# Block-sum copies on SyncE's queue, one y store, earlier sums in a hybrid decoder block

## The chip, the cores and the metric

The kernel runs on one core of a Trainium2 chip. The metric is the device time of one execution in microseconds (us). TensorE (PE) multiplies; VectorE (DVE), ScalarE (ACT) and GpSimd (POOL) do the element-wise work; SyncE (SP), ACT and POOL issue transfers (DMA) between DRAM and the core's memory, or between two places in DRAM.

## The reference

```python
h = concat(meta_tokens, x)                                  # 16 + 1024 tokens, 1024 wide
n = rmsnorm(h, norm_g)
u, z_pool, q, k, v, z_attn, f, g_pool, g_attn = split(n @ w_in[0])
y_pool = causal_multiscale_pool(u, pool_w, pool_scale) * silu(z_pool)      # 4 groups of 128, windows 2, 4, 8, 16
log_f  = log_sigmoid(f + b_forget)
y_attn = forgetting_attention(q, k, v, log_f) * silu(z_attn)               # 8 heads of 64, causal softmax
merged = sigmoid(g_pool) * (y_pool @ w_up_pool[0]) + sigmoid(g_attn) * (y_attn @ w_up_attn[0])
out = rmsnorm(h + merged @ w_out[0], final_norm_g)[16:]
```

All arrays are float32. The kernel keeps that precision by splitting each operand into a high and a low part and adding three products (high x high, high x low, low x high).

## The kernel before, in words

Work runs in stages: loading and normalising x (to about 20 us), the first q, k and v projections (to 60), attention merged with projections (64 to 430), a product of blocks of h with columns of w_in in seven block products instead of eight (430 to 550), the up projections (to 637), and the output projection, again in seven block products (to 714).

**Attention** has 16 units: head pairs p = 0 to 3, head e of a pair, half of the queries. A unit with 5 or 9 key blocks computes scores and adds the forget term (`L710`, `L715`), takes the maxima with a transpose at `L729`, and then for each key block subtracts the maximum, takes the exponential (`L752`), splits it into `ph` and `pl` (`L756`, `L757`) and multiplies with V (`L775`). The scores of the next unit stand among the soft blocks of this one. Between those steps PE works on projections that nothing waits for yet: `f_u(3, 2, 1, 0)`, then eight `gp` and four `ga` columns (`f_raw`). Each loads a raw weight of 512 KB (`raw`, `L151`), splits it into `whi` (ACT, `L156`) and `wlo` (POOL, `L158`), multiplies (`L170`) and evicts its result through `st` (ACT, `L357` and `L347`) to DRAM (`sp_u`, `sp_gp`, `sp_ga`, by SP). The pool of `st` has two buffers: an eviction into it waits until the store of the one but last has landed.

**Block sums.** The two stages with seven products need sums of blocks: TD of w_out (512x512), GS of w_in (512x768) and HS of h, where hi and lo parts are added or the negated block (`neg`) is subtracted. They are built in DRAM while attention runs: a copy puts one block in place (`put`, pieces of 512 KB), and an accumulating DMA that POOL issues adds another (`add`, `L616`). The table `SUMS` says after which unit's transposes which copies are queued and which add is issued. ACT issues the copies, in `move` (`L612`), between an exponential and the following `ph`; in the soft blocks of a unit its queued copies are spread. SP stores the negated blocks (`L609`), the sums of exponentials (`accd`, `L607`) and, at a unit's end, the two halves of the unit's output `t` as `y` and `y2` (`L788`, 128 KB each). When both heads of a pair are done, POOL adds `y2` to `y` (`add_y`, `L643`). The sum of p = 0 is issued at i = 5, of p = 1 at i = 9, of p = 2 at i = 13.

**Order.** PE's order is written by hand. The order on ACT, DVE, POOL and SP is set when the program is built, from the dependencies and from `after(...)` and `behind(...)`; each engine then works its list strictly in order, and each queue of DMAs likewise starts them in order. An instruction waits by semaphores for what it reads and for the buffers that it writes. DMAs share a small set of semaphores, so a DMA's issue can also wait for an earlier DMA that used the same one.

Of the kernel before, what the change touches and what calls it, by code (L numbers as in the profile page):

```python
# [8 lines left out]
F32 = mybir.dt.float32  # L9
# [7 lines left out]
SEQ = 1024  # L17
# [9 lines left out]
COL_U, COL_Z, COL_Q, COL_K, COL_V, COL_ZA = 0, 512, 1024, 1536, 2048, 2560  # L27
# [17 lines left out]
def r32(ap):  # L45
    return ap.bitcast(F32)
# [7 lines left out]
def tile_hybrid_block(ctx, tc, x, meta, norm_g, w_in, b_forget, pool_w, pool_scale,  # L54
# [84 lines left out]
    def tt(out, x, y, op, eng):  # L139
        if eng is nc.gpsimd:  # L140
            pool_tt(out, x, y, op)
        else:
            eng.tensor_tensor(out, x, y, op=op)

    los = []

    def split_w(srcs, pool=None, tags=("wh", "wl")):
        raw = wp.tile([128, KO, 128], F32, name="raw")
        k0 = 0
        for s in srcs:  # L150
            nc.sync.dma_start(raw[:, k0:k0 + s.shape[1], :], s)  # L151
            k0 += s.shape[1]
        hi = (pool or wp).tile([128, KO, 128], F32R, name="whi", tag=tags[0])
        lo = (pool or wp).tile([128, KO, 128], F32R, name="wlo", tag=tags[1])
        for k in range(0, KO, 4):
            nc.scalar.activation(hi[:, k:k + 4], raw[:, k:k + 4], AF.Copy)  # L156
# [83 lines left out]
    def rows(e):  # L240
        return slice(64 * e, 64 * e + 64), slice(64 - 64 * e, 128 - 64 * e)
# [230 lines left out]
    for n, (kind, t0, t1) in enumerate(todo):  # L472
        if n + 4 < 8:
            xts[n + 4] = norm_load(n + 4)
        if kind == "q":
            run(q_piece(0, wq, t0, t1))
        elif kind == "k":
            run(k_piece(0, wk, t0, t1))
        else:
            g = v_piece(0, wv, t0, t1)  # L480
            run(g)
        i = {0: 2, 1: 3, 3: 4, 4: 5, 5: 8, 6: 6, 7: 7}.get(n)
        if i is not None:
            norm_t(i, xts[i], ntok(i))
        if n == 0:
            hv_ = split_hi(rv, gp, "g")
            wv = split_lo(rv, hv_, gp, "g")
            VT[0] = gp.tile([128, L], F32, name="vt", tag="g")
            v_alloc(0)
        i = {1: 4, 2: 5, 3: 8, 4: 6, 5: 7}.get(n)  # L490
        if i is not None:
            norm_scale(xts[i], ntok(i), norm_stat(xts[i], ntok(i)))
        if n == 2:
            zero_q(0)
        if n == 4:
            wf = at_.tile([128, KO, H], F32, name="wf", bufs=1)
            nc.sync.dma_start(wf, w_in2[:, :, COL_F:COL_F + H])
        if n == 8:
            wfs = at_.tile([128, KO, 2 * H], F32R, name="wfs", bufs=1)
            nc.vector.tensor_copy(wfs[:, :, :H], wf)  # L500
            nc.vector.tensor_tensor(wfs[:, :, H:], wf, r32(wfs[:, :, :H]), op=ALU.subtract)
        if n in (4, 7, 10):
            run(v_blocks(0, *range(max(1, 2 * (n // 3) - 2), 2 * (n // 3))))
    G_.close()
# [71 lines left out]
    TD = {n: dr.tile([512, 512], F32, name=f"td{n}") for n in (1, 2, 3, 4, 5)}  # L576
    WB = {"11": w_out[0][:512, :512], "12": w_out[0][:512, 512:], "21": w_out[0][512:, :512], "22": w_out[0][512:, 512:]}

    GS = {n: dr.tile([512, 768], F32, name=f"gs{n}") for n in (1, 2, 3, 4, 5)}
    GB = {f"{r + 1}{c + 1}": (w_in[0][512 * r:512 * r + 512, z:z + 512], w_in[0][512 * r:512 * r + 512, g:g + 256])  # L580
          for r in range(2) for c, (z, g) in enumerate(((COL_ZA, COL_GA + 512), (COL_Z, COL_GA + 768)))}
    for j in range(4, 8):
        spill["ga", j] = dr.tile([128, SEQ], F32, name=f"sp_ga{j}")
    HS = {n: dr.tile([512, 512], F32, name=f"hs{n}") for n in ("11", "22", "l11", "l22", "A", "B", "C", "X")}

    accs = []

    def hblock(d, blk):
        r, c = int(blk[0]) - 1, int(blk[1]) - 1
        return r32(d[c][:, :, 512 * r:512 * r + 512])  # L590

    def rows_of(t):
        return t.rearrange("(k p) c -> p k c", p=128)

    puts, held, negs = [], [], []

    def put(dst, src):
        for r in (0, 256):
            puts.append((dst[r:r + 256], src[r:r + 256]))

    def put_g(dst, src):
        put(dst[:, :512], src[0])
        puts.append((dst[:, 512:], src[1]))

    def move(u, b):
        if b == 2 and held:
            nc.sync.dma_start(*held.pop(0))  # L607
        while b == 3 and negs:
            nc.sync.dma_start(*negs.pop(0))  # L609
        if b:  # L610
            for _ in range(-(-len(puts) // (u.nb - b))):
                after(nc.scalar.dma_start(*puts.pop(0)), exps[-1])  # L612

    def add(dst, src):
        d, r = [t.rearrange("r c -> (r c)").rearrange("(p m) -> p m", m=2048) for t in (dst, src)]
# [1 line left out]

    trs = []

    def put_h(n):  # L620
        for d, h in ((HS[n], hh4), (HS["l" + n], hl4)):
            for k in (0, 2):
                puts.append((rows_of(d)[:, k:k + 2], hblock(h, n)[:, k:k + 2]))

    def put_neg(blk, k, *dsts):
        t = ap_.tile([128, 512], F32, name="neg", bufs=1)
        after(nc.scalar.activation(t, hblock(hh4, blk)[:, k], AF.Copy, scale=-1.0), exps[-1])
        for c in range(0, 512, 256):
            sub = nc.gpsimd.tensor_tensor(t[:, c:c + 256], t[:, c:c + 256], hblock(hl4, blk)[:, k, c:c + 256],
                                          op=ALU.subtract)  # L630
            after(sub, accs[-1])
        for d in dsts:
            negs.append((HS[d][128 * k:128 * k + 128], t))

    def n21(k):
        put_neg("21", k, "X", "A")

    def n12(k):
        put_neg("12", k, "C")

    def add_y(p):
        d, r = [spill[n, p].rearrange("(p k) c -> p (k c)", k=2) for n in ("y", "y2")]
        behind(nc.gpsimd.dma_start(d, r, accum_op=ALU.add, max_dma_last_dim=8192), trs[-1])  # L643
# [18 lines left out]

    def sums_of(i):
# [11 lines left out]
    class Unit:  # L675
# [69 lines left out]
        def soft(self, b):  # L745
# [4 lines left out]
                self.acc = ap_.tile([KB, 512], F32, name="acc", bufs=2)  # L750
            nc.vector.tensor_tensor(s[:kb, c0:], s[:kb, c0:], self.pm[:kb, c0:], op=ALU.subtract)  # L751
            exps.append(nc.scalar.activation(s[:kb, c0:], s[:kb, c0:], AF.Exp))  # L752
# [3 lines left out]
            nc.scalar.activation(ph[:kb, c0:], s[:kb, c0:], AF.Copy)  # L756
# [33 lines left out]

    def merged(a, c):
# [697 lines left out]
```

## Time and profile before

| what | us |
|---|---|
| median of the runs | 721.78 (721.3 to 722.93) |
| profiled execution | 722.44, of it span 720.4 |
| mean granted clock of PE in it | 0.996 |
| PE busy | 707.4 (98% of the span) |
| DVE, ACT, POOL busy | 512.0 (71%), 425.9 (59%), 353.9 (49%) |

The span runs from the first to the last instruction of the profiled execution; its own time is 2.04 longer. A row of a timeline reads: start, duration, engine and line, operation with output and inputs, shape, count, and in brackets the idle time in front of it with what ended it. An engine name with q (ACTq, SPq) is that engine's issue of a DMA, not the transfer. Durations of matmuls include their pipeline, so consecutive ones overlap.

### The profile page before, as it was taken

What the parts mean: (1) busy time and instruction counts of PE and PEld (TensorE: products, weight loads), DVE (VectorE), ACT (ScalarE), POOL (GpSimd) and SP (SyncE); (2) the same over time, 40 slices, a digit from 0 to 9 for tenths busy, and PEclk for the clock granted to TensorE, in tenths of its full rate; (3) what the DMA queues carried; (4) which work ended last, traced back from release to release, by engine and by line L of the source; (5) the groups of instructions that cost most, each with busy time, mean ns of one, the idle gap of its engine ahead of it and who ended that gap; (6) DMA issues with size and microseconds to landing.
All of it is one profiled execution on the core that took longest, in us unless ns stands there. A gap on an engine that the chain in (4) does not pass through costs nothing.

```text
span 720.4 us, 10921 instructions
## 1 busy us (share of the span) xinstructions
PE 707.4 (98%) x3613; PEld 610.7 (85%) x3613; DVE 512.0 (71%) x909; ACT 425.9 (59%) x936; POOL 353.9 (49%) x481
## 2 busy tenths in 40 slices
PE   8999999799999999999999999999999999999996
PEld 6997999798889988898888888888888888888885
DVE  5743488477688767787587866899847545888775
ACT  7753577567787867777587614455646332535445
POOL 5412336477377675747388643458951010007152
PEclk9999999999999999999999999999999999999999
DMA  9211225986968889497858768799518366861006
GB/s 308 65 30 30 60 62 199 271 244 193 260 177 230 239 229 281 118 261 214 224 154 206 223 202 318 239 304 308 129 35 273 113 224 233 272 224 60 0 1 233
DMA packets 97482, 134.09 MB, mean 186 GB/s; under 512 B 11809, under 2 KB 63009, under 8 KB 95154
## 3 DMA queue, kind: packets, MB, share of 16 engines
q1 hardware_dynamic: 83296, 94.07, 40.8%
q0 software_dynamic: 2512, 18.35, 13.3%
q10 hardware_dynamic: 11618, 20.98, 8.2%
q8 instruction: 28, 0.46, 0.2%
q14 instruction: 28, 0.23, 0.1%
HBM read 103.29 MB, written 62.59 MB: 230 GB/s over the span
## 4 chain that ended last, share of the span: by engine, by line
PE 94%; ACT 2%; DMA 2%; DVE 1%; issue 1%; POOL 0%; POOLq 0%; ACTq 0%
PE pj L170 55%; PE pj L1049 12%; PE pj L1369 8%; PE po L775 5%; PE pt L1049 4%; PE pt L1369 2%; PE ps L711 2%; DMA sp_u<-st 2%; PE ps L710 2%; PE pj L521 1%; PE pt L232 1%; PE pj L711 1%; PE pj L710 1%; ACT qa L268 1%; PE pn L232 0%
## 5 line engine op out<-in xcount | busy, mean ns | idle before, releaser
L170 PE MATMUL pj<-hh,whi 128*128 128x512 f32 (+3 forms) x576 | 128.3, 350 | 0.0
L170 PE MATMUL pj<-hh,wlo 128*128 128x512 f32 (+3 forms) x576 | 127.1, 346 | 0.0
L170 PE MATMUL pj<-hl,whi 128*128 128x512 f32 (+3 forms) x576 | 126.8, 345 | 0.0
L170 PEld LDWEIGHTS pj<-hh,whi 128*128 128x128 f32 x576 | 98.4, 190 | 10.2 <-ACT hh L234 0.4
L158 POOL TENSOR_TENSOR wlo<-raw,whi 128x256 fp32r<-128x256 f32 x100 | 73.5, 774 | 65.1 <-PE pj L170 24.5
L170 PEld LDWEIGHTS pj<-hh,wlo 128*128 128x128 f32 x576 | 96.8, 188 | 10.0
L765 POOL TENSOR_TENSOR acc<-acc,S 128x256 f32<-128x256 f32 (+2 forms) x128 | 90.3, 723 | 30.5 <-ACT S L752 20.8
L170 PEld LDWEIGHTS pj<-hl,whi 128*128 128x128 f32 x576 | 96.6, 189 | 9.8
L757 DVE TENSOR_TENSOR pl<-S,ph 128x512 fp32r<-128x512 f32 (+4 forms) x112 | 80.5, 736 | 19.4 <-ACT ph L756 18.9
L1011 POOL TENSOR_TENSOR gw<-graw,gw 128x256 fp32r<-128x256 f32 x52 | 53.6, 1056 | 44.2 <-ACT gw L1004 41.8
L1049 PE MATMUL pj<-gh,gw 128*128 128x512 f32 x276 | 64.3, 389 | 0.0
L724 DVE TENSOR_TENSOR pt<-pt,S 128x400 f32<-128x400 f32 (+2 forms) x96 | 46.4, 483 | 22.1 <-ACT S L715 19.6
L1049 PEld LDWEIGHTS pj<-gh,gw 128*128 128x128 f32 x276 | 51.8, 188 | 10.9
L752 ACT ACTIVATE S<-S 128x512 f32<-128x512 f32 (+4 forms) x112 | 50.6, 479 | 8.6 <-DVE S L751 8.4
L756 ACT ACTIVATE ph<-S 128x512 fp32r<-128x512 f32 (+4 forms) x112 | 52.4, 482 | 2.3 <-PE po L775 1.4
L751 DVE TENSOR_TENSOR S<-S,pt 128x512 f32<-128x512 f32 (+4 forms) x112 | 49.7, 498 | 0.6
L1262 DVE TENSOR_TENSOR rl<-pj,rl 128x512 f32<-128x512 f32 x32 | 22.0, 689 | 28.7 <-PE pj L170 28.1
L1004 ACT ACTIVATE gw<-graw 128x512 fp32r<-128x512 f32 x38 | 23.5, 626 | 27.9 <-DMA graw<-gs 12.0
L715 ACT ACTIVATE S<-ps,negc 128x16 f32<-128x16 f32 (+4 forms) x65 | 33.0, 513 | 10.9 <-PE ps L711 10.3
L765 POOL TENSOR_TENSOR acc<-S 128x256 f32<-128x256 f32 (+1 forms) x32 | 28.6, 926 | 21.1 <-ACT S L752 17.5
L136 POOL TENSOR_TENSOR X<-G 128x256 f32<-128x256 f32 x8 | 5.8, 740 | 63.9 <-DVE G L1264 63.9
L775 PE MATMUL po<-ph,V 128*128 128x512 f32 (+4 forms) x112 | 36.6, 327 | 0.3 <-ACT ph L756 0.2
(250 smaller groups left out, 1434.2 us busy)
## 6 DMA issues: line engine op xcount, KB each, us to landing
raw<-in_w_in_dram SPq DMA_DIRECT2D x27, 512.0 KB, 5.9
gs<-in_w_in_dram ACTq DMA_DIRECT2D x15, 512.0 KB, 7.6
gs<-gs POOLq DMA_DIRECT2D x4, 1536.0 KB, 12.7
graw<-gs SPq DMA_DIRECT2D x12, 512.0 KB, 6.1
td<-in_w_out_dram ACTq DMA_DIRECT2D x10, 512.0 KB, 11.4
graw<-in_w_in_dram SPq DMA_DIRECT2D x9, 512.0 KB, 6.9
xt<-in_x_dram SPq DMA_DIRECT2D x8, 512.0 KB, 6.3
accd<-acc SPq DMA_DIRECT2D x16, 256.0 KB, 4.2
```

Source lines behind the costliest of these rows:

```text
L158: ins = nc.gpsimd.tensor_tensor(lo[:, k:k + 2], raw[:, k:k + 2], r32(hi[:, k:k + 2]), op=ALU.subtract)
L170: nc.tensor.matmul(ps, a, b, start=(i == 0), stop=(i == len(seq) - 1))
L724: nc.vector.tensor_tensor(m[:kb, c0:], m[:kb, c0:], s[:kb, c0:], op=ALU.max)
L751: nc.vector.tensor_tensor(s[:kb, c0:], s[:kb, c0:], self.pm[:kb, c0:], op=ALU.subtract)
L752: exps.append(nc.scalar.activation(s[:kb, c0:], s[:kb, c0:], AF.Exp))
L756: nc.scalar.activation(ph[:kb, c0:], s[:kb, c0:], AF.Copy)
L757: dves.append(nc.vector.tensor_tensor(pl[:kb, c0:], s[:kb, c0:], r32(ph[:kb, c0:]), op=ALU.subtract))
L765: accs.append(nc.gpsimd.tensor_tensor(acc[:kb, c:c1], (S0 if b == 1 else acc)[:kb, c:c1], s[:kb, c:c1], op=ALU.add))
L775: nc.tensor.matmul(self.po[:, c0:], v, self.P[b][i][:kb, c0:], start=(b == 0 and i == 0), stop=(b == self.nb - 1 and i == 1))
L1011: nc.gpsimd.tensor_tensor(op[:, 1, k:k + 2], raw[:, k:k + 2], r32(op[:, 0, k:k + 2]), op=ALU.subtract)
L1049: nc.tensor.matmul(ps, stat(n, i, p, k), op_h[n][q][k // 2][:, k % 2], start=fresh and m == 0, stop=m == 11, skip_group_check=True)
L1369: nc.tensor.matmul(ps, pick(A_, k, p)[:, i * 128:(i + 1) * 128], pick(B_, k, q)[:, c0:c1], start=start and n == 0, stop=n == 11, skip_grou ...
```

## The change

The 33 copies of 512 KB are issued by SP: six in the loop that loads x, one for each step n > 5, and three behind each of the first nine raw weights that `split_w` loads, `after` that load. ACT issues none of them. The order of the copies is a list written at the head. The adds of `SUMS` move up: GS1 += GS5 now stands at unit 0, and the rest follow in the order of the table; none is left for i = 14. The two halves of a unit's output, one above the other in `t`, are stored by one DMA of 128x512 into a 256-row `sp_y` (p < 3), and `add_y` adds rows 64 to 191 of it to rows 0 to 63 and 192 to 255, by a list of 2 x 32 rows. The negated block 21 is written by one DMA to both halves of `XA` (X and A, stacked), and B is made by one copy of A by SP. `attn_in` loads y by two DMAs where p < 3.

```diff
...
+    XA = dr.tile([1024, 512], F32, name="hsXA")
+    HS["X"], HS["A"] = XA[:512], XA[512:]
...
+    def copies(n, prev=None):
+        for _ in range(min(n, len(puts))):
+            ins = nc.sync.dma_start(*puts.pop(0))
+            if prev is not None:
+                after(ins, prev)
+
+    put_g(GS[5], GB["12"])
+    put_g(GS[1], GB["11"])
+    put_h("11")
+    put_h("22")
+    put_g(GS[3], GB["22"])
+    put(TD[5], WB["12"])
+    put(TD[1], WB["11"])
+    put_g(GS[2], GB["11"])
+    put(TD[3], WB["22"])
+    put_g(GS[4], GB["21"])
+    put(TD[2], WB["11"])
+    put(TD[4], WB["21"])
...
     def split_w(srcs, pool=None, tags=("wh", "wl")):
         raw = wp.tile([128, KO, 128], F32, name="raw")
         k0 = 0
         for s in srcs:
-            nc.sync.dma_start(raw[:, k0:k0 + s.shape[1], :], s)
+            load = nc.sync.dma_start(raw[:, k0:k0 + s.shape[1], :], s)
             k0 += s.shape[1]
+        copies(3, load)
...
+        if n > 5:
+            copies(1)
...
-        for n in ("y", "y2"):
-            spill[n, p] = dr.tile([128, SEQ], F32, name=f"sp_{n}{p}")
+        spill["y", p] = dr.tile([128 if p == 3 else 256, SEQ], F32, name=f"sp_y{p}")
...
-        if b:
-            for _ in range(-(-len(puts) // (u.nb - b))):
-                after(nc.scalar.dma_start(*puts.pop(0)), exps[-1])
...
-        for d in dsts:
-            negs.append((HS[d][128 * k:128 * k + 128], t))
+        r = slice(128 * k, 128 * k + 128)
+        if blk == "21":
+            negs.append((XA.rearrange("(n q) c -> q n c", n=2)[r], t[:, None, :].to_broadcast([128, 2, 512])))
+        else:
+            negs.append((HS["C"][r], t))
...
     def add_y(p):
-        d, r = [spill[n, p].rearrange("(p k) c -> p (k c)", k=2) for n in ("y", "y2")]
+        v = spill["y", p].rearrange("(n p k) c -> n p (k c)", n=4, k=2)
+        d, r = v[0::3], v[1:3]
         behind(nc.gpsimd.dma_start(d, r, accum_op=ALU.add, max_dma_last_dim=8192), trs[-1])
 
+    def put_b():
+        negs.append((HS["B"], HS["A"]))
+
     SUMS = {
-        0: [(put_h, "11")],
-        1: [(add, HS["11"], HS["l11"]), (n21, 0), (put, TD[1], WB["11"]), (put, TD[5], WB["12"])],
-        2: [(add, TD[1], TD[5]), (n21, 1), (put_h, "22")],
-        3: [(add, HS["22"], HS["l22"]), (n21, 2), (put, TD[3], WB["22"])],
-        4: [(add, TD[3], TD[5]), (n21, 3), (put_g, GS[1], GB["11"])],
-        5: [(add, HS["X"], HS["11"]), (n12, 0), (put_g, GS[5], GB["12"])],
-        6: [(add, HS["A"], HS["22"]), (n12, 1), (put_g, GS[3], GB["22"])],
-        7: [(add, GS[1], GS[5]), (n12, 2), (put, HS["B"], HS["A"])],
-        8: [(add, HS["B"], HS["11"]), (n12, 3), (put_g, GS[2], GB["11"])],
-        9: [(add, GS[3], GS[5]), (put, TD[2], WB["11"])],
-        10: [(add, HS["C"], HS["B"]), (put_g, GS[4], GB["21"])],
-        11: [(add, GS[2], GS[3]), (put, TD[4], WB["21"])],
+        0: [(add, GS[1], GS[5]), (n21, 0)],
+        1: [(add, HS["11"], HS["l11"]), (n21, 1)],
+        2: [(add, HS["22"], HS["l22"]), (n21, 2)],
+        3: [(add, GS[3], GS[5]), (n21, 3)],
+        4: [(add, TD[1], TD[5]), (n12, 0)],
+        5: [(add, HS["X"], HS["11"]), (n12, 1)],
+        6: [(add, HS["A"], HS["22"]), (n12, 2)],
+        7: [(add, GS[2], GS[3]), (n12, 3)],
+        8: [(add, TD[3], TD[5]), (put_b,)],
+        9: [(add, HS["B"], HS["11"])],
+        10: [(add, HS["C"], HS["B"])],
+        11: [(add, GS[4], GS[2])],
         12: [(add, TD[2], TD[3])],
-        13: [(add, GS[4], GS[2])],
-        14: [(add, TD[4], TD[2])],
+        13: [(add, TD[4], TD[2])],
...
-            move(self, b)
+            move(b)
...
-            for n, part in (("y", hr), ("y2", lr))[:1 if self.p == 3 else 2]:
-                nc.sync.dma_start(spill[n, self.p][hr, self.q0:self.q0 + 512], t[part])
+            if self.p == 3:
+                nc.sync.dma_start(spill["y", 3][hr, self.q0:self.q0 + 512], t[hr])
+            else:
+                nc.sync.dma_start(spill["y", self.p][128 * self.e:128 * self.e + 128, self.q0:self.q0 + 512], t)
...
-        nc.sync.dma_start(y, spill["y", p])
+        if p == 3:
+            nc.sync.dma_start(y, spill["y", p])
+        else:
+            for e in range(2):
+                nc.sync.dma_start(y[rows(e)[0]], spill["y", p].rearrange("(n r) c -> n r c", n=4)[3 * e])
...
```

On SP, unit 0's end: before, a raw load is followed by the halves of y and the stores of the second `f_u` (`sp_u_1348`).

```order
L151 DMA raw<-in_w_in_dram 128x8x128
L788 DMA sp_y_773<-t 64x512
L359 DMA sp_u_1348<-st 128x384
L788 DMA sp_y_774<-t 64x512
L359 DMA sp_u_1348<-st 128x384
L359 DMA sp_u_1348<-st 128x256
L359 DMA sp_u_1348<-st 128x16
```

Three copies of 512 KB (`gs`, `L179`) now stand between this raw load and the stores (here `sp_u_1361`); y is one row.

```order
L202 DMA raw<-in_w_in_dram 128x8x128
L179 DMA gs_133<-in_w_in_dram 256x512 x2
L179 DMA gs_133<-in_w_in_dram 512x256
L817 DMA sp_y_796<-t 128x512
L411 DMA sp_u_1361<-st 128x384 x2
L411 DMA sp_u_1361<-st 128x256
L411 DMA sp_u_1361<-st 128x16
```

The stores of the projection stand behind the copies in the one queue; their own order is the same.

On ACT, in the soft blocks of unit 0, the third eviction of that `f_u` (128x272) and what stands behind it. Before:

```order
L357 ACTIVATE st<-pj 128x272
L752 ACTIVATE S<-S 128x512
L612 DMA hsl_797<-hl_124 128x2x512
L756 ACTIVATE ph<-S 128x512
L715 ACTIVATE S<-ps,negc 128x272
L752 ACTIVATE S<-S 128x512
L612 DMA hsl_797<-hl_124 128x2x512
L756 ACTIVATE ph<-S 128x512
L715 ACTIVATE S<-pj,negc 128x144
L752 ACTIVATE S<-S 128x400
L752 ACTIVATE S<-S 128x272
L756 ACTIVATE ph<-S 128x400
```

And now:

```order
L409 ACTIVATE st<-pj 128x272
L779 ACTIVATE S<-S 128x16
L783 ACTIVATE ph<-S 128x512
L872 ACTIVATE pwh<-raw 128x512
L648 ACTIVATE neg<-hh_123 128x512
L208 ACTIVATE whi<-raw 128x512
L742 ACTIVATE S<-ps,negc 128x272
L783 ACTIVATE ph<-S 128x400
L208 ACTIVATE whi<-raw 128x512
L742 ACTIVATE S<-pj,negc 128x144
L783 ACTIVATE ph<-S 128x272
```

The DMAs are gone; the eviction stands later in the unit's soft blocks, with the last three wide `ph` and the splits behind it.

On POOL, i = 5, where X and the sum of y for p = 0 are issued. Before:

```order
L629 TENSOR_TENSOR neg<-neg,hl_126 128x256 x2
L158 TENSOR_TENSOR wlo<-raw,whi 128x256 x4
L616 DMA hsX<-hs_795 128x2048
L643 DMA sp_y_773<-sp_y_774 64x2048
L762 COPY acc<-S 128x112
```

And now:

```order
L650 TENSOR_TENSOR neg<-neg,hl_126 128x256 x2
L210 TENSOR_TENSOR wlo<-raw,whi 128x256 x4
L636 DMA hsXA<-hs_137 128x2048
L668 DMA sp_y_796<-sp_y_796 2x32x2048
L789 COPY acc<-S 128x112
```

The place is the same; the list of the second add is 2 x 32 rows instead of 64.

More of the change, by code (lines that the diff above doesn't have):

```diff
@@ L143, in tt, with hblock, rows_of, put @@
             eng.tensor_tensor(out, x, y, op=op)
+    TD = {n: dr.tile([512, 512], F32, name=f"td{n}") for n in (1, 2, 3, 4, 5)}
+    WB = {"11": w_out[0][:512, :512], "12": w_out[0][:512, 512:], "21": w_out[0][512:, :512], "22": w_out[0][512:, 512:]}
+    GS = {n: dr.tile([512, 768], F32, name=f"gs{n}") for n in (1, 2, 3, 4, 5)}
+    GB = {f"{r + 1}{c + 1}": (w_in[0][512 * r:512 * r + 512, z:z + 512], w_in[0][512 * r:512 * r + 512, g:g + 256])
+          for r in range(2) for c, (z, g) in enumerate(((COL_ZA, COL_GA + 512), (COL_Z, COL_GA + 768)))}
+    HS = {n: dr.tile([512, 512], F32, name=f"hs{n}") for n in ("11", "22", "l11", "l22", "B", "C")}
+    XA = dr.tile([1024, 512], F32, name="hsXA")
+    HS["X"], HS["A"] = XA[:512], XA[512:]
+    def hblock(d, blk):
+        r, c = int(blk[0]) - 1, int(blk[1]) - 1
+        return r32(d[c][:, :, 512 * r:512 * r + 512])
+    def rows_of(t):
+        return t.rearrange("(k p) c -> p k c", p=128)
+    puts, held, negs = [], [], []
+    def put(dst, src):
+        for r in (0, 256):
+            puts.append((dst[r:r + 256], src[r:r + 256]))
+    def put_g(dst, src):
+        put(dst[:, :512], src[0])
+        puts.append((dst[:, 512:], src[1]))
+    def put_h(n):
+        for d, h in ((HS[n], hh4), (HS["l" + n], hl4)):
+            for k in (0, 2):
+                puts.append((rows_of(d)[:, k:k + 2], hblock(h, n)[:, k:k + 2]))
+    def copies(n, prev=None):
[15 more added lines that the diff above has]
+    put(TD[4], WB["21"])
     los = []
@@ L572, in tile_hybrid_block, with add, move @@
     for p in range(4):
-        for n in ("y", "y2"):
-            spill[n, p] = dr.tile([128, SEQ], F32, name=f"sp_{n}{p}")
[L576 to L581, printed above, removed]
+        spill["y", p] = dr.tile([128 if p == 3 else 256, SEQ], F32, name=f"sp_y{p}")
     for j in range(4, 8):
         spill["ga", j] = dr.tile([128, SEQ], F32, name=f"sp_ga{j}")
-    HS = {n: dr.tile([512, 512], F32, name=f"hs{n}") for n in ("11", "22", "l11", "l22", "A", "B", "C", "X")}
     accs = []
[L588 to L605, printed above, removed]
+    def add(dst, src):
+        d, r = [t.rearrange("r c -> (r c)").rearrange("(p m) -> p m", m=2048) for t in (dst, src)]
+        behind(nc.gpsimd.dma_start(d, r, accum_op=ALU.add, max_dma_last_dim=8192), trs[-1])
+    trs = []
+    def move(b):
         if b == 2 and held:
@@ L609, in move, with put_neg @@
             nc.sync.dma_start(*negs.pop(0))
-        if b:
-            for _ in range(-(-len(puts) // (u.nb - b))):
-                after(nc.scalar.dma_start(*puts.pop(0)), exps[-1])
-    def add(dst, src):
-        d, r = [t.rearrange("r c -> (r c)").rearrange("(p m) -> p m", m=2048) for t in (dst, src)]
-        behind(nc.gpsimd.dma_start(d, r, accum_op=ALU.add, max_dma_last_dim=8192), trs[-1])
[L618 to L625, printed above, removed]
+    def put_neg(blk, k):
         t = ap_.tile([128, 512], F32, name="neg", bufs=1)
@@ L631, in put_neg @@
             after(sub, accs[-1])
-        for d in dsts:
-            negs.append((HS[d][128 * k:128 * k + 128], t))
+        r = slice(128 * k, 128 * k + 128)
[3 more added lines that the diff above has]
+            negs.append((HS["C"][r], t))
     def n21(k):
-        put_neg("21", k, "X", "A")
+        put_neg("21", k)
     def n12(k):
-        put_neg("12", k, "C")
+        put_neg("12", k)
```

## The prediction

> **What bounds the kernel now.** I read the page first: the busy time of each engine and the chain that ended last.
>
> ```profile
> PE 707.4 (98%) x3613; PEld 610.7 (85%) x3613; DVE 512.0 (71%) x909; ACT 425.9 (59%) x936; POOL 353.9 (49%) x481
> ...
> q1 hardware_dynamic: 83296, 94.07, 40.8%
> q0 software_dynamic: 2512, 18.35, 13.3%
> q10 hardware_dynamic: 11618, 20.98, 8.2%
> ...
> PE 94%; ACT 2%; DMA 2%; DVE 1%; issue 1%; POOL 0%; POOLq 0%; ACTq 0%
> ```
>
> TensorE works for 98% of the span and carries 94% of the chain. The change leaves PE's order as it was, so it can pay only where PE waits. The middle three rows are the DMA queues: packets, MB, share of 16 engines' span. q1 carries what SP issues, q10 what ACT issues, q0 the adds of POOL. The second view is what PE waited for (us in total, times, longest):
>
> ```profile
> PE pj L710 <- ACT S L715: 4.1, 1, 4.1
> PE pn L419 <- DVE car L557: 1.3, 1, 1.3
> ```
>
> There is one wait worth having. The chain of waits, from 125 to 142 us, says what stood behind it, and the timelines of ACT and PE and the stretches around it (busy time of PE, PEld, DVE, ACT, POOL, then granted clock and DMA share) give its size:
>
> ```profile
> 128.03 11.14 DMA sp_u<-st
> ...
> 139.19 0.50 ACTq L612
> ```
> ```profile
> 139.79 0.69 ACT L715 ACTIVATE S<-pj,negc 128x512 f32<-128x512 f32 x1 [7.55 <-DMA sp_u<-st]
> ```
> ```profile
> 140.53 0.50 PE L710 MATMUL pj<-qa,ka 128*128 128x512 f32 x1 [4.11 <-ACT S L715]
> ```
> ```profile
> 136.00:141.00 5.00, 0.89 (x5) 0.52 (x4) 0.00 (x0) 1.21 (x3) 0.22 (x1) 1.00 1.01 351
> 141.00:145.00 4.00, 4.00 (x15) 3.73 (x14) 2.10 (x3) 3.28 (x7) 1.12 (x2) 0.57 1.05 314
> ```
>
> In unit 2's prefix ACT issued the third copy of `td` (L612) only at 139.19, when a store of `sp_u` issued at 128.03 had landed 11.14 us later. ACT stood still for 7.55 us, the eviction S behind that copy was late, and PE idled 4.11 us. For the next 4 us the granted clock was 0.57, which costs 4.00 x 0.43 = 1.7. The DMA engines were full (1.01, 1.05): the store was slow because the queue was.
>
> **The change, part by part. Removed.** No copy stands on ACT any more, so this stall cannot come back in this form: 4.11 + 1.7 = 5.8 us gained. Bounds: 5.8 if nothing takes its place; hardly more, since PE's next wait is 1.3, at L419, where nothing changes. The 33 issues taken from ACT (0.50 each, as the 139.19 row) are 16 us on an engine that is 59% busy: nothing on the path.
>
> **Moved: three copies behind each raw load on SP.** Now SP's queue, in order, holds raw, three copies, then y and the `sp_u` stores. What each takes of 16 engines comes from the queue rows and the span, 720.4 us: q1 0.408 x 720.4 / 94.07 = 3.1 us a MB, q10 (the copies) 2.8, q0 (the adds) 0.133 x 720.4 / 18.35 = 5.2. The landing times of `sp_u` by its tile, and the sizes in KB with median times to landing by the list of DMA issues:
>
> ```profile
> DMA to landing us min/median/max: 1.9/4.5/12.0
> ```
> ```profile
> raw<-in_w_in_dram SPq DMA_DIRECT2D x27, 512.0 KB, 5.9
> gs<-in_w_in_dram ACTq DMA_DIRECT2D x15, 512.0 KB, 7.6
> gs<-gs POOLq DMA_DIRECT2D x4, 1536.0 KB, 12.7
> ...
> sp_u<-st SPq DMA_DIRECT2D x8, 192.0 KB, 2.7
> sp_y<-sp_y POOLq DMA_DIRECT2D x3, 512.0 KB, 13.3
> ```
>
> A raw load is 0.52 MB, 1.6 us; three copies 4.4; a whole y store 0.8; a `sp_u` store of 384 columns 0.6; a GS add 8.2. The add counts in full ahead of what is issued after it, because the engines serve the queues in turn, packet by packet. In 224 to 226, with an add of y under way:
>
> ```profile
> q0 software_dynamic: 45, 0.37, 88.3%
> q10 hardware_dynamic: 43, 0.09, 11.3%
> q1 hardware_dynamic: 44, 0.02, 5.6%
> ```
>
> 45 packets against 43 and 44, but an add's packet (8 KB) takes 0.883 x 32 / 45 = 0.63 us and the others 0.08 and 0.04. While an add lasts, SP's queue moves one packet for each 0.63 us.
>
> Units 0 and 1. The timelines of before: SP's raw load in each unit, then ACT's and PE's rows of unit 0:
>
> ```profile
> 105.54 0.38 SPq L151 DMA_DIRECT2D raw<-in_w_in_dram  x1
> ```
> ```profile
> 125.36 0.38 SPq L151 DMA_DIRECT2D raw<-in_w_in_dram  x1
> ```
> ```profile
> 115.76 0.38 ACT L357 ACTIVATE st<-pj 128x272 f32<-128x272 f32 x1
> 116.04 0.62 ACT L752 ACTIVATE S<-S 128x512 f32<-128x512 f32 x1
> 116.69 0.63 ACT L756 ACTIVATE ph<-S 128x512 fp32r<-128x512 f32 x1
> ```
> ```profile
> 120.74 0.39 PE L775 MATMUL po<-ph,V 128*128 128x512 f32 x1
> ...
> 122.87 0.37 PE L775 MATMUL po<-ph,V 128*128 128x272 f32 x1
> ```
>
> Unit 0: after the change the add GS1 += GS5 starts here too, right behind the unit's first steps on POOL. Ahead of the end of u2's first store lie 1.6 + 4.4 + 0.8 + 0.6 + 8.2 = 15.6 us of work from 105.54, and 1.3 for issue and landing (the shortest `sp_u` store took 1.9 from issue to landing, 0.6 of it work): 122.4. `st` has two buffers, so ACT's third eviction of u2 (115.76 now) waits until then, 6.6 us, and behind it stand, in ACT's order, S, ph 512, pwh, neg, whi, S, ph 400, whi, S and ph 272, at some 0.47 from start to start (115.76 to 116.69, two steps). Then ph 512 starts at 123.3 and ends at 124.0 where PE wants it at 120.74 (3.2 late); ph 272, ten steps behind the eviction, starts at 127.1 and ends at 127.5 against 122.87, 4.6 in all. Bounds: 0, if the store gets through ahead of the copies; 6.6, the whole wait of ACT. I take 4.5. Each piece is shorter than the 4.11 behind which the clock fell, so I add nothing for the clock.
>
> Unit 1. Behind the raw of 125.36 now come the store of both negated blocks, three copies and then u1's first store, with the add of `hs` (1.05 MB, 5.5 us) beside them: 1.6 + 1.6 + 4.4 + 0.6 + 5.5 = 13.7, again 1.3. The raw itself waits for a buffer that PE sets free, 4.5 later than now: 125.36 + 4.5 + 15.0 = 144.9; ACT's third eviction of u1 waits for it, and PE can start 1 us later (S of 139.79 to PE at 140.53, rounded up), at 145.9 if all lines up at its worst. PE would run dry at 136.42 + 4.5 = 140.9, the old start of its idle time moved. So 5.0 at most; if the raw load isn't held back, the store lands 4.5 sooner and 0.5 is left. I take the middle, 2.8, and nothing for the clock; bounds 0.5 and 6.7, with the clock. Unit 2 has one copy ahead of u0's first store instead of three; 0, with 4 as the upper bound.
>
> SP's one store of y, XA written once (a broadcast read of `neg`) and the moved TD and GS adds: each is the same bytes as now or fewer, their readers stand after the last unit in SP's order, and no PE wait shown stands behind them: 0. Loading y in two pieces: 0, for the same reason.
>
> **The adds of y.** Before, 64 rows of 8 KB; now the list reads 2 x 32 x 2048. All the adds of the trace have lists of 192, 128 or 64 rows, which are multiples of 16, and they spread over all engines. No row shows what a first number of 2 does. If the rows are dealt by all 64, the price is 0. If by the first number, two engines get 32 packets each instead of 4: with the 8 of the add issued just ahead, and one packet of another queue between any two, 40 x (0.63 + 0.08) = 28 us. Every transfer of SP has a share on these two engines and is held until then. Three places; POOL's issues, SP's raw load, ACT's splits and PE's matmul that the first (i = 5) and the last (i = 13) touch, in before:
>
> ```profile
> 219.22 1.04 POOL L643 DMA_DIRECT2D sp_y<-sp_y  x1
> ```
> ```profile
> 382.55 1.08 POOL L643 DMA_DIRECT2D sp_y<-sp_y  x1
> ```
> ```profile
> 386.13 0.38 SPq L151 DMA_DIRECT2D raw<-in_w_in_dram  x1
> ```
> ```profile
> 248.94 0.62 ACT L156 ACTIVATE whi<-raw 128x512 fp32r<-128x512 f32 x1
> ```
> ```profile
> 404.10 0.62 ACT L156 ACTIVATE whi<-raw 128x512 fp32r<-128x512 f32 x1
> ```
> ```profile
> 406.98 0.39 PE L775 MATMUL po<-ph,V 128*128 128x512 f32 x1
> ```
>
> The raw of 386.13 would land at 382.55 + 2.5 (an estimate of an add's start: 12.7 for a GS add less 8.2 leaves 4.5 for start and landing) + 28 = 413. ACT's whi waits for it, and the next ph stand behind whi, wanted by PE at 406.98: 6.0 us, longer than 4.11, so 1.7 more for the clock. At i = 5 the same sum ends at 219.22 + 2.5 + 28 = 249.7, 0.8 after the next raw is to be split (248.94); I take 0.5, and as much at i = 9, where raw loads stand as far from the add; bounds 0 and 3 each. So 8.7, between 0 and 14.
>
> I take the second, dealt by the first number: the changed shape is the only thing that differs from the adds in the trace, and their evenness needs nothing but a first number that 16 divides.
>
> By the Trainium skill, "DMA: Bandwidth & Descriptors", the section "Why a DMA increments its semaphore by 16 and not by 1", the number of engines is the largest up to 16 that divides the slowest dimension longer than 1. It would put this add on two engines and speaks against the change; no run here shows it yet, the even spread of 64, 128 and 192 rows fits it. By the skill's "TensorE: Matmul & The Clock Gate", Part 1, an idle window of about 3.4 us halves the clock; the trace agrees, with 0.57 after 4.11 us. By that rule the 3.2 at unit 0 stays just below, and if it did not, 1.7 would be added.
>
> **Sum**, against the profiled execution (span 720.4, 722.44 in all): 722.44 - 5.8 + 4.5 + 2.8 + 8.7 = 732.6. The median of the runs shown, 721.78, stands 0.66 below it: 732.0, the forecast.
>
> **The rivals.**
>
> Late stores, but y's adds spread as before: 722.44 - 5.8 + 7.3 - 0.66 = 723.3. For it: the bytes and the packets are the same as now. Against it: the order of the shape.
>
> The stall is simply gone, on the faster side: 721.78 - 5.8 = 716.0, up to 719 with a wait of 3 us left at one unit. It decides if u2's and u1's first stores land before ACT wants `st` again, that is, if the copies start late or the engines take turns in a way that lets a 0.6 us store pass, and the y adds spread. For it: the median `sp_u` store took 4.5 and ACT's blocks are long, so a store may pass in time where raw and copies start sooner than I reckon. Against it: one queue works in order, and the three copies are ahead in it.
>
> Only the y adds bite: 721.78 - 5.8 + 8.7 = 724.7.
>
> Worse: everything above, and the clock falls at unit 0, at unit 1 and at all three y adds: 732 + 4 x 1.7 (i = 13 has its own already) + 4 for the upper bounds of the waits at units 0 and 1: 743. For it: the 3.2 of unit 0 is not far from 4.11. Against it: five falls of the clock where there was one.
>
> **How the numbers follow.** Late stores and slow y adds 0.42 (732, from 725 to 739 for itself); late stores alone 0.19 (723.3, from 718 to 727); stall gone 0.22 (716 to 719); y adds alone 0.10 (724.7); worse 0.07 (743). About 0.2%, 1.4 us, is what a measurement of this kernel tells from no change. Stall gone gives faster 0.21, same 0.01. Late stores alone: slower 0.10, same 0.06, faster 0.03. The likeliest: slower 0.41, faster 0.01. Y adds alone: slower 0.08, same 0.02. Worse: slower 0.07. In all: faster 0.25, same 0.09, slower 0.66. The range is 715.5 to 740; it leaves out about 0.05 below and 0.1 above.
>
> **What would show it.** Right: ACT waits before `st` (the third eviction of u2 and of u1) for DMA `sp_u<-st`, with PE's ph or S matmuls behind; no wait on a copy; the adds of y take 25 us or more from issue to landing where they took 13.3, and ACT's whi<-raw near 404 waits for its raw. Wrong: y's adds near 13 us again (then about 8 us fewer); `sp_u` stores landing in 5 us at units 0 and 1 (then 7 fewer); or a PE wait elsewhere, above all around 430, where products read the sums.

## The result and the profile after

| | median, us | runs | ratio to before |
|---|---|---|---|
| before | 721.86 | 721.3 to 722.93 | |
| after | 753.15 | 750.57 to 756.92 | 1.0436 (1.0378 to 1.0494) |

The change makes the kernel 31 us slower; 732 was forecast, with 740 as the upper end. The direction is right, the size is three times the forecast's. The profiled execution has a span of 755.2, 34.8 more than before.

The page of the kernel after: busy times, DMA queues and the chain.

```profile
PE 718.6 (95%) x3613; PEld 618.1 (82%) x3613; DVE 510.1 (68%) x909; ACT 423.8 (56%) x936; POOL 352.9 (47%) x481
...
q1 hardware_dynamic: 93376, 112.42, 46.6%
q0 software_dynamic: 3856, 18.36, 13.0%
q10 hardware_dynamic: 1298, 2.63, 0.9%
```

The copies have moved from q10 to q1 (20.98 to 2.63 MB, 94.07 to 112.42). PE is busy 11.2 us longer with the same 3613 matmuls: part of the loss is a slower clock. What PE waited for, in the kernel after:

```profile
PE po L802 <- ACT ph L783: 17.9, 5, 9.4
PE pj L737 <- ACT S L742: 4.2, 2, 2.4
PE pj L1082 <- DVE gx L1093: 3.2, 1, 3.2
```

One wait of 4.1 has become several. They are in PE's timeline, with the idle time in brackets:

```profile
125.36 0.80 PE L802 MATMUL po<-ph,V 128*128 128x512 f32 x1 [3.46 <-ACT ph L783]
...
144.33 0.50 PE L737 MATMUL pj<-qa,ka 128*128 128x512 f32 x1 [1.77 <-ACT S L742]
152.69 0.59 PE L737 MATMUL pj<-qa,ka 128*128 128x272 f32 x1 [2.39 <-ACT S L742]
...
255.92 0.50 PE L802 MATMUL po<-ph,V 128*128 128x512 f32 x1 [1.84 <-ACT ph L783]
...
340.70 0.79 PE L802 MATMUL po<-ph,V 128*128 128x512 f32 x1 [2.81 <-ACT ph L783]
...
435.07 0.79 PE L802 MATMUL po<-ph,V 128*128 128x512 f32 x1 [9.38 <-ACT ph L783]
...
518.01 2.47 PE L1082 MATMUL pj<-gh,gw 128*128 128x512 f32 x5 [3.16 <-DVE gx L1093]
```

The first three are units 0 to 2. The next three stand at the ends of the adds of y, issued at 225.83, 310.50 and 400.23 and landed 29.6 to 30.0 us later. The last stands in the seven products. Behind most of them the granted clock falls; the stretches (columns as in the prediction):

```profile
125.00:129.00 4.00, 3.64 (x14) 3.41 (x14) 2.39 (x5) 4.00 (x11) 3.25 (x5) 0.58 0.43 127
...
146.00:150.00 4.00, 4.00 (x16) 3.68 (x15) 0.94 (x2) 0.09 (x1) 1.10 (x2) 0.64 1.06 342
...
153.00:157.00 4.00, 4.00 (x19) 3.90 (x19) 3.84 (x13) 1.46 (x6) 0.00 (x0) 0.66 1.00 341
...
341.00:346.00 5.00, 5.00 (x17) 4.61 (x17) 4.94 (x7) 4.16 (x10) 4.75 (x6) 0.50 0.79 187
...
435.00:440.00 5.00, 4.93 (x14) 3.90 (x15) 4.95 (x7) 4.09 (x10) 5.00 (x6) 0.60 0.39 125
```

What stood in front of PE's waits, on ACT:

```profile
124.29 0.40 ACT L409 ACTIVATE st<-pj 128x272 f32<-128x272 f32 x1 [6.71 <-DMA sp_u<-st]
...
151.57 0.49 ACT L409 ACTIVATE st<-pj 128x384 f32<-128x384 f32 x1 [5.47 <-DMA sp_u<-st]
...
244.76 0.60 ACT L813 ACTIVATE t<-po 128x512 f32<-128x512 f32 x1 [2.33 <-DMA sp_y<-t]
...
431.69 1.15 ACT L208 ACTIVATE whi<-raw 128x512 fp32r<-128x512 f32 x2 [10.62 <-DMA raw<-in_w_in_dram]
```

And the adds of y, in the list of DMA issues (median to landing: 13.3 before), and the queues from 235 to 240, in the middle of the first:

```profile
sp_y<-sp_y POOLq DMA_DIRECT2D x3, 512.0 KB, 29.8
```
```profile
q0 software_dynamic: 32, 0.11, 11.2%
```

In that stretch all the DMA work of the add is 11.2% of 16 engines, the time of 1.8 of them, with 0.11 MB moved in 5 us: two engines work and fourteen stand. The trace shows it in another way too. It keeps the sixteen steps in which a transfer's landing is counted. Of the first add, issued at 225.83, fourteen steps had come by 235.54, the last two at 255.35 and 255.43. The store of y that SP issued at 227.35 had fourteen by 235.37, the other two at 244.24 and 244.68; the raw load of 410.42 had fourteen by 414.57, the other two at 431.48 and 431.59. Two late steps of sixteen, in the add and in the transfers that end with it, fit two engines of sixteen that are held up.

Where the 34.8 us of span went can be counted by the start of each of PE's 3613 matmuls: the time to the next start above the median for its shape, summed by stretch, after less before. 100 to 160 (units 0 to 2, with the old stall gone): 7.3. 220 to 280: 5.5. 320 to 360: 5.8. 420 to 440: 11.3. 500 to 520: 4.4. The rest is 0.5. The three stretches of the adds make 22.6.

### The profile page after: what moved, and what is told of

Its sections match the earlier page's. It is cut to its first block, busy times and chain, and to the rows that moved or that the text cites. A ratio compares the mean times of both kernels' runs of the same rounds, so it can differ in the third digit from the quotient of the medians.

```text
span 755.2 us, 10903 instructions
## 1 busy us (share of the span) xinstructions
PE 718.6 (95%) x3613; PEld 618.1 (82%) x3613; DVE 510.1 (68%) x909; ACT 423.8 (56%) x936; POOL 352.9 (47%) x481
## 3 DMA queue, kind: packets, MB, share of 16 engines
q1 hardware_dynamic: 93376, 112.42, 46.6%
q10 hardware_dynamic: 1298, 2.63, 0.9%
## 4 chain that ended last, share of the span: by engine, by line
PE 58%; DMA 8%; DVE 5%; ACT 4%; issue 2%; POOL 1%; SPq 1%; POOLq 0%; ACTq 0%; DVEq 0%
PE pj L222 33%; PE pj L1402 8%; PE pj L1082 6%; PE po L802 4%; DMA zp<-accd 3%; DMA raw<-in_w_in_dram 3%; PE pt L1402 2%; PE pt L1082 2%; DMA sums<-ge 1%; POOL acc L792 1%; PE ps L738 1%; PE ps L737 1%; DVE pl L784 1%; ACT S L742 1%; DVE zp L993 1%
## 5 line engine op out<-in xcount | busy, mean ns | idle before, releaser
L222 PE MATMUL pj<-hh,wlo 128*128 128x512 f32 (+3 forms) x576 | 129.3, 350 | 0.0
L222 PE MATMUL pj<-hl,whi 128*128 128x512 f32 (+3 forms) x576 | 128.6, 348 | 0.0
L222 PEld LDWEIGHTS pj<-hh,wlo 128*128 128x128 f32 x576 | 98.9, 192 | 10.4
L1044 POOL TENSOR_TENSOR gw<-graw,gw 128x256 fp32r<-128x256 f32 x52 | 49.9, 986 | 50.8 <-ACT gw L1037 49.7
L802 PE MATMUL po<-ph,V 128*128 128x512 f32 (+4 forms) x112 | 38.8, 347 | 18.1 <-ACT ph L783 17.9
L208 ACT ACTIVATE whi<-raw 128x512 fp32r<-128x512 f32 x50 | 29.5, 624 | 22.1 <-DMA raw<-in_w_in_dram 13.6
L802 PEld LDWEIGHTS po<-ph,V 128*128 128x128 f32 x112 | 22.3, 199 | 21.9 <-ACT ph L783 20.1
```

Of the source, the lines that this page charges most:

```text
L222: nc.tensor.matmul(ps, a, b, start=(i == 0), stop=(i == len(seq) - 1))
L802: nc.tensor.matmul(self.po[:, c0:], v, self.P[b][i][:kb, c0:], start=(b == 0 and i == 0), stop=(b == self.nb - 1 and i == 1))
L1044: nc.gpsimd.tensor_tensor(op[:, 1, k:k + 2], raw[:, k:k + 2], r32(op[:, 0, k:k + 2]), op=ALU.subtract)
```

## The experiments

Two theories were set against each other. One: the adds of y, dealt to two engines by the first number of their list, are the greater part, and the copies ahead of the `sp_u` stores the lesser. The other: SP's fuller queue does it all, and the adds are slow because it is full. A third thing was not thought of beforehand: another list can also change the order in which the engines' lists are built.

**The list of y's adds with its two dimensions swapped.**

```diff
-        d, r = v[0::3], v[1:3]
+        d, r = [x.rearrange("n p m -> p n m") for x in (v[0::3], v[1:3])]
```

> The changed kernel, with the list of y's adds read as 32 x 2 x 2048 instead of 2 x 32 x 2048: same rows, same bytes, the two dimensions swapped. Theory (the adds are dealt over engines by the first number): the add lands in about 13 us instead of 29.8, PE's losses at 246 to 257, 337 to 345 and 425 to 439 go (5.5 + 5.8 + 11.3 = 22.6 us more than in the kernel before), and the time is 753 - 22.6 = about 730; 726 if the 4.4 us at 514 also comes from it. Rival (it is SP's fuller queue, not the adds): landing still near 30 or the same losses, 745 or more.

734.67 us, ratio 1.0162 (1.0140 to 1.0184), against 1.0436 with the change as it was: 2.7% or 20 us back, for the same rows and bytes in another order. The adds land in 11.8 us (13.3 before the change), and all sixteen steps of the first come between 235.14 and 236.25:

```profile
sp_y<-sp_y POOLq DMA_DIRECT2D x3, 512.0 KB, 11.8
```

PE's waits at 255 (1.84), 340 and 435 are gone; what is left is the units' and a smaller wait in the products:

```profile
PE pj L737 <- ACT S L742: 4.4, 2, 2.4
PE po L802 <- ACT ph L783: 3.1, 1, 3.1
...
PE pj L1082 <- DVE gx L1093: 1.2, 1, 1.2
```

The time is some 3 above the 730 expected if before is set at the 723.57 that it took on that chip (a ratio of 1.0162 is 11.7 us). The products' wait shrank from 3.2 to 1.2, and one of 1.6 at 274, on S behind a store of `sp_gp`, took its place among the longest.

This run does not change the transfer alone. In the two traces the order of instructions on ACT and DVE differs, in the three stretches of the adds and nowhere else (ACT, in the changed kernel: 236 to 276, 319 to 353, 402 to 442). At i = 9 the changed kernel has the last scores and the maxima (`mx`) behind `whi`:

```profile
329.20 1.15 ACT L208 ACTIVATE whi<-raw 128x512 fp32r<-128x512 f32 x2 [1.31 <-issue]
...
331.79 0.38 ACT L742 ACTIVATE S<-ps,negc 128x144 f32<-128x144 f32 x1
...
335.91 0.37 ACT L763 ACTIVATE mx<-pt 64x16 f32<-64x16 f32 x2 [0.74 <-DVE pt L761]
```

With the swapped list they stand ahead of it, as in the kernel before:

```profile
319.50 0.38 ACT L742 ACTIVATE S<-ps,negc 128x144 f32<-128x144 f32 x1 [0.17 <-PE ps L738]
...
323.89 0.37 ACT L763 ACTIVATE mx<-pt 64x16 f32<-64x16 f32 x2 [0.34 <-DVE pt L761]
...
326.01 1.15 ACT L208 ACTIVATE whi<-raw 128x512 fp32r<-128x512 f32 x2
```

So the run shows that the shape of the list costs the 20 us. It does not tell how much of that is the slow transfer and how much the other order; why the order came out so is not on record.

**Only y changed, in the kernel before.** The store, the add (2 x 32 x 2048) and the load of y as in the change; copies on ACT and the other adds where they were.

```diff
-        d, r = [spill[n, p].rearrange("(p k) c -> p (k c)", k=2) for n in ("y", "y2")]
+        v = spill["y", p].rearrange("(n p k) c -> n p (k c)", n=4, k=2)
+        d, r = v[0::3], v[1:3]
```

> The kernel before with only y changed: one store of both halves, the add as 2 x 32 x 2048, y loaded in two pieces; copies and the other adds stay on ACT and where they were. Theory: the adds land in 25 us or more, and the time rises by the same 22.6 us or some less, since ACT's queue carries part of the load: 738 to 746. Rival (the adds hurt only together with SP's copies): 722 to 726.

768.66 us, ratio 1.0628 (1.0605 to 1.0651): 45 us slower, twice what was expected and worse than the whole change. The rival is out: the list does harm without SP's copies. The adds land after 32.9, 36.6 and 33.1 us, later than in the change (29.6 to 30.0), and PE's two longest waits are

```profile
247.05 0.66 PE L307 MATMUL ps<-ident,vt 128*128 128x128 f32 x2 [8.58 <-DVE S L719]
```
```profile
449.62 0.79 PE L775 MATMUL po<-ph,V 128*128 128x512 f32 x1 [18.21 <-ACT ph L756]
```

Parts do not add up: y alone costs 45, the rest alone 8 (below), both 31. In this kernel the second and third adds of y stand behind GS adds of 1.5 MB instead of 1 MB adds, and copies are under way on ACT's queue at the first two; that these make the difference was not tried. The order on ACT and DVE differs here too from that of the kernel before, at the three adds.

**Lists of 2, 4 and 8.** The kernel before, with blocks of y and y2 alternating in DRAM so that the three adds have lists of 2 x 32, 4 x 16 and 8 x 8 rows; y's stores and loads are more and smaller.

```diff
+        v = spill["y", p].rearrange("r c -> (r c)").rearrange("(n s p m) -> s n p m", n=2 << p, s=2, m=2048)
+        d, r = v[0], v[1]
```

> The kernel before, with y's three adds as lists of 2 x 32, 4 x 16 and 8 x 8 rows of 8 KB (blocks of y and y2 alternate in DRAM, so that the lists stay of two levels), with more and smaller stores of y. Theory (dealt by the first number): landing 29 to 33 us for the first; 16 packets on each of 4 engines behind the 12 of a GS add, some 22 to 24, for the second; 8 and 12, some 17 to 18, for the third. Rival (any list of two levels goes to two engines): about 30 or more for all three.

751.96 us in its one run. The three adds, in the list of DMA issues of a stretch around each:

```profile
sp_y<-sp_y POOLq DMA_DIRECT2D x1, 512.0 KB, 32.7
```
```profile
sp_y<-sp_y POOLq DMA_DIRECT2D x1, 512.0 KB, 24.4
```
```profile
sp_y<-sp_y POOLq DMA_DIRECT2D x1, 512.0 KB, 16.1
```

32.7, 24.4, 16.1 for the same 512 KB. As many of the sixteen steps of landing come late as the list's first number says: of the list of 2, two (fourteen by 231.79, two at 251.48 and 251.71); of 4, four (twelve by 328.83, four from 338.15 to 338.40); of 8, eight (eight by 419.80, eight from 424.50 to 424.81). So the number of engines follows the first number. The rule of the Trainium skill, "DMA: Bandwidth & Descriptors", section "Why a DMA increments its semaphore by 16 and not by 1", is what the runs show here.

**Nine copies behind the first three raw loads.** As the swapped list, and the copies earlier.

```diff
-        copies(3, load)
+        copies(9, load)
```

> As e1_swap, and the copies stand nine behind each of the first three raw loads (before 60 us) instead of three behind nine. Theory (late stores at units 0 to 2 come from copies ahead of them): the waits at 121, 142 and 150 go or shrink to the add's part, and the time falls from e1_swap's by 5 to 13 us, to about 717 to 725. Rival (the adds alone hold the stores): no change from e1_swap beyond 2.

727.23 us, ratio 1.0047 (1.0029 to 1.0066), 8 below the swapped list alone. Of the three waits of PE at units 0 to 2, two are 0.27 and 0.50 now and the third is gone: the copies ahead of the stores made them, at unit 0 together with the add (next run). Something new came: the fourth raw load now stands behind nine copies, as the chain shows,

```profile
76.39 12.18 DMA raw<-in_w_in_dram
```

and costs some 2.8 between 95 and 104: here too the copies hold up what SP issues next.

**The add of unit 0 moved to unit 14.** As the swapped list, with GS1 += GS5 at the end.

```diff
-        0: [(add, GS[1], GS[5]), (n21, 0)],
+        0: [(n21, 0)],
+        14: [(add, GS[1], GS[5])],
```

> As e1_swap, with the add GS1 += GS5 moved from unit 0 to unit 14. Theory (the add's 8.2 us counts in full ahead of u2's first store): the wait at 121 (3.6 us and 1.8 for the clock) goes, and the time falls by some 5 from e1_swap's. Rival (the copies alone make it late): the same within 1.

733.82 us, ratio 1.0138 (1.0114 to 1.0162), not apart from the swapped list's 1.0162. Neither theory fits whole. ACT's two evictions and PE's one wait:

```profile
117.95 0.40 ACT L409 ACTIVATE st<-pj 128x272 f32<-128x272 f32 x1 [0.83 <-DMA sp_u<-st]
142.46 0.40 ACT L409 ACTIVATE st<-pj 128x272 f32<-128x272 f32 x1 [8.18 <-DMA sp_u<-st]
```
```profile
145.35 0.80 PE L738 MATMUL pj<-qa,ka 128*128 128x512 f32 x1 [8.39 <-ACT S L743]
```

The add did hold u2's store: without it ACT waits 0.83, with it 6.38 in the swapped list's run. But then PE reaches unit 1 sooner, while u1's first store still stands behind raw, XA and three copies, and PE waits there for 8.39 instead of 1.99 and 2.39. The loss moved by one unit; and with the add at the end, the products' wait is 2.8 instead of 1.2.

**y wholly as before.** The change without its y part: copies on SP and moved adds only.

```diff
-        v = spill["y", p].rearrange("(n p k) c -> n p (k c)", n=4, k=2)
-        d, r = v[0::3], v[1:3]
+        d, r = [spill[n, p].rearrange("(p k) c -> p (k c)", k=2) for n in ("y", "y2")]
```

> The changed kernel with y wholly as before: two stores of 128 KB, the add as 64 x 2048, one load a pair. What is left of the change is the copies on SP and the moved adds. Theory (y's layout also cost the 1.4 us that e1_swap still loses at 492, through the second y load on SP ahead of the sums): that loss goes, 733 or 1.5 below e1_swap. Rival (that loss has to do with the copies or the sums): as e1_swap, 734.7, with the wait of PE on DVE gx still above 1.

731.26 us, ratio 1.0112 (1.0090 to 1.0134), 8 above before. PE has no wait on DVE's gx in the products any more, so that wait came with y's layout. The order on ACT and DVE is that of the swapped list. In the changed kernel the chain to PE's start at 518.01 runs through SP: the issues of y's two loads (0.45 and 0.60 us from 499.26), those of `graw` (0.59 and 0.51), then `sums`, 8.78 us to landing. The second load of y is 0.60 of it; the load of y was not tried apart.

**The copies 12, 12 and 3.** As y wholly as before, with most copies behind two raw loads.

```diff
-        copies(3, load)
+        copies(12, load)
```

> As e6_ybefore, with the copies 12, 12 and 3 behind the first three raw loads. Theory (in e3_swap_c9 nine copies behind the third raw load held the fourth for 12.18 us, 2.8 us lost at 95 to 103; y's second load 1.4 at 486): both go, 723, the same as the kernel before; 721 if the wait for sp_gp at 266 goes as well. Rival (the copies are in the way wherever SP issues them): 727 or more.

730.28 us, ratio 1.0106 (1.0079 to 1.0132): a miss, and the rival's case. The waits at units 0 to 2 shrank, but the third raw load, issued behind twelve copies at 65.47, took 12.50 us to land, and PE waited for the q projection made of it:

```profile
83.22 2.90 PE L222 MATMUL pj<-hh,whi 128*128 128x384 f32 x8 [5.34 <-DVE ql L324]
```

Packed together, the copies only move their price.

**The adds of units 7 and 8 exchanged.** As y wholly as before.

```diff
-        7: [(add, GS[2], GS[3]), (n12, 3)],
-        8: [(add, TD[3], TD[5]), (put_b,)],
+        7: [(add, TD[3], TD[5]), (n12, 3)],
+        8: [(add, GS[2], GS[3]), (put_b,)],
```

> As e6_ybefore, with the adds of units 7 and 8 exchanged: TD3 += TD5 (1 MB) at 7, GS2 += GS3 (1.5 MB) at 8. Theory (a sp_gp store is held for 11.94 us by the GS add of unit 7 and the eviction behind it costs 2.3 at 274): the wait goes and the time falls by 2 from e6_ybefore. Rival (the raw load and the y stores there hold it): no change, or the same wait a unit later.

729.88 us, ratio 1.0083 (1.0066 to 1.0100), and its interval overlaps that of y wholly as before. PE's wait for S at 275 went from 1.5 to 0.7, the store of `sp_gp` from 11.94 to 11.15 us: the size of the add can have a part in it, no more. The two times cannot be told apart.

**One part of the change alone: the four copies of TD1 and TD5 early on SP.** In the kernel before, they are issued in the x loop; all else stays, but for a few places in the order on ACT and DVE between 129 and 158.

```diff
+        if n > 5 and early:
+            nc.sync.dma_start(*early.pop(0))
...
-        1: [(add, HS["11"], HS["l11"]), (n21, 0), (put, TD[1], WB["11"]), (put, TD[5], WB["12"])],
+        1: [(add, HS["11"], HS["l11"]), (n21, 0)],
```

> The kernel before with one part of the change alone: the four copies of TD1 and TD5, which ACT issued in unit 1 and the stall stood behind, issued by SP in the x loop (n > 5, some 17 to 20 us), where the DMA engines are nearly idle. All else as before. Theory (the copies on ACT and the traffic that they made at 129 were the stall, 5.8 us with the clock): ACT's next wait at st is short, PE's 4.1 goes, and the time is 716 to 718, some 5 below before. Rival (the sp_u store is late anyway, and ACT's third eviction of u1 waits for it in place of the copy): within 1.4 of before.

717.49 us (before: 723.41 beside it), ratio 0.9917 (0.9903 to 0.9932): 6.0 us faster than before, and the best kernel here. PE's longest wait is now the one of 1.3 that stood second before:

```profile
PE pn L424 <- DVE car L564: 1.3, 1, 1.3
```

and the stretch of the old stall is full of work, at full clock, though the DMA engines are as busy as they were:

```profile
136.00:141.00 5.00, 5.00 (x27) 4.64 (x26) 1.56 (x3) 4.17 (x8) 3.97 (x6) 1.00 1.02 288
141.00:145.00 4.00, 4.00 (x28) 3.96 (x27) 3.90 (x13) 1.94 (x7) 0.00 (x0) 1.00 1.07 340
```

## Why the prediction was wrong, step by step

**What bounds it, and what is removed: right.** The old stall was worth 5.8 us by the prediction; taken away alone it gave 6.0.

**Late stores at units 0 and 1: right mechanism, too small.** ACT's wait for u2's store was forecast as 6.6 and is 6.71; PE's first wait as 3.2 and is 3.46. ACT's third eviction of u1, at 141.43, did wait for u1's first store, issued at 131.29 and landed at 141.34. The waits of PE add up to 7.6 (3.46, 1.77, 2.39) where the sum had 7.3, but by luck: the three terms were 4.5, 2.8 and 0. "I add nothing for the clock" failed: behind 3.46 the clock was 0.58 for 4 us (1.7), and behind 1.77 and 2.39 it was 0.64 and 0.66 (1.4 each). The old stall's 4.11 was the only case that the trace before had, and I took it for a threshold that no row showed. With the old stall's gain in it, units 0 to 2 come to +7.3 where the sum had -5.8 + 7.3 = 1.5.

**The adds of y: right choice of the two ends, wrong size, and this is the step that failed most.** 2.5 + 28 us to the end of the add was forecast, 29.6 to 30.0 measured. 8.7 us of loss was forecast, 22.6 counted, 20 by the swapped list. What failed is that the three places were read from the timelines of before, as if only the landing of the next raw load could come later.

At i = 13 (11.3) I ended the wait with that landing. The load had landed at 431.59 and ACT went on at 431.69, but PE started at 435.07: two `whi`, two S, an eviction and the `ph` itself stood between, 3.4 us, so 9.38 for 6.0. The order was another one here too: in the kernel before and with the swapped list two of the unit's `ph` stand ahead of the first `whi` (401.86 and 403.04, then 404.10, before the change); in the changed kernel both `whi` stand ahead of all of them.

At i = 5 and i = 9 (5.5 and 5.8), "I take 0.5, and as much" failed by more. A store was held too: ACT's `t` at 244.76 waited 2.33 for the store of y. But ACT then waited 1.37 more for PE (`vt` at 246.73), so this did not decide. The chain to PE's waits at 255.92 and 340.70 holds no transfer at all back to 225 and 310. It runs over ACT and DVE in their new order: at i = 5 the last scores S stand behind `vt` and `t` (247.12; with the swapped list at 236.53), at i = 9 behind `whi`, `t` and `ka` (331.79; 319.50). These two losses came with the order that the program got with the new list, which the prediction took as unchanged, and not, as far as the chain shows, from waiting for the two engines. And the clock fell again, at i = 9 (0.50 from 341 to 346) and at i = 13 (0.60 from 435 to 440).

**Loading y in two pieces, at 0: wrong.** "No PE wait shown stands behind them" was true of the trace before. 4.4 us were lost at 514 (3.16 and the clock); 1.2 of wait with the swapped list, none with y as before. So part came from y's layout and the rest with the slow adds; the chain shows SP's issues on the way, but not why they came so late.

**The rivals.** "Only the y adds bite" named the greater part and, like the forecast, made it too cheap. The worse case, 743 with a chance of 0.07, was the closest. The rival on the faster side needed stores ahead of copies and spread adds; neither came.

**What the range missed.** Its upper end, 740, held the bound of 14 us for the adds of y, below the 22.6. That bound was built on three raw loads, and not on the order on ACT and DVE.

## What to carry to other kernels

When an address list is given a new outer dimension, look at its first number before anything else: a list of 2 x 32 rows moved 512 KB in 30 us where 32 x 2 took 12, and held the transfers behind it on the same engines. Compare the built order of each engine before and after as well: here it changed with the list. A copy that is needed late does harm by standing in front of what is needed soon. The four copies that stood in the way, issued at 17 to 20 us instead, gave 6 us (in the kernel before the DMA share was 1.00 from 16 to 20, so not idle, but 0.70 to 24 and 0.00 from 24 to 30). Moving all 33 to the common queue, with the adds moved up, cost 8. Price a wait to the instruction that PE wants, not to the transfer's landing, and add the clock.

## What the runs showed of the hardware

The granted clock fell behind waits of PE as short as 1.77 us in the kernel after, but not behind 1.84. The half-clock stretches of this trace begin at 124.98, 145.46, 152.29, 340.02, 428.77 and 517.52: 0, 6, 8, 63, 89 and 115 steps of 3.413 us from the first. By these figures, what counts is how much of the idle time falls into one such slot. The wait of 1.77 lies in one, with PE busy for 1.64 us, and the next slot has half the clock; the wait of 1.84 is split over two, the emptier with 2.05 busy, and the clock stays:

```profile
142.05:145.46 3.41, 1.64 (x9) 1.23 (x8) 0.00 (x0) 3.38 (x8) 3.20 (x6) 1.00 1.01 318
145.46:148.88 3.42, 3.42 (x11) 3.14 (x10) 1.40 (x2) 0.63 (x2) 1.64 (x3) 0.50 1.07 339
...
254.69:258.10 3.41, 2.05 (x8) 1.40 (x9) 3.09 (x8) 3.41 (x8) 2.78 (x4) 1.00 0.80 163
258.10:261.51 3.41, 3.41 (x18) 2.89 (x17) 3.41 (x7) 3.25 (x7) 3.41 (x4) 1.00 0.62 165
```

With the swapped list the wait of 2.39 at 151.68 is split too (2.07 and 2.35 busy) and cost no clock, where the same 2.39 in the kernel after did. So a wait near 2 us costs the clock or not by where it falls. Of the slots at full clock in this trace, those with 1.64 us or less of PE are followed by half the clock, those with 2.05 or more are not; one slot of the run with only y changed (1.49, from 429.93) goes the other way, so the busy time of the view is not the whole rule. The page "TensorE: Matmul & The Clock Gate" of the Trainium skill, Part 1, gives an idle window of about 3.4 us; in this trace 1.77 and 2.39 were enough, so the measurement decides against reading it as a least idle time.

The accumulating DMA whose list starts with 2 keeps two engines busy while the other fourteen stand, and the transfers of another queue wait for their share on these two: from 235 to 245, after the change, the mean DMA share is 0.14, and the store of y that SP had issued at 227.35 landed at 244.68.

```profile
235.00:245.00 10.00, 9.62 (x58) 9.18 (x57) 4.87 (x12) 4.23 (x13) 7.68 (x12) 1.00 0.14 30
```

Here a low DMA share does not mean that transfers are fast.
